# Two blocks on one core: matmuls that fill a part of the array, issued beside others on another part

## The chip, the cores and the metric

The kernel runs on one core of a Trainium2 chip. The metric is device time in microseconds (us), the median of several executions. The profile is one further execution, recorded instruction by instruction. PE is the matmul engine, PEld its weight loads, DVE, ACT and POOL the three other compute engines, SP the queue that issues the DMAs.

## The reference

Two network blocks follow each other on 256 tokens of width 1024, in float32. What the change touches, cut from the reference:

```python
m_l = silu(c) @ w_ada + b_ada                 # modulation of x, 1024 -> 6144
m_c = silu(c_ctx) @ w_ada + b_ada             # modulation of the context
u_l = modulate(x, sh1_l, sc1_l) @ w_in        # LN, scale, shift, projection; u_c likewise
...
la = log_sigmoid(r @ w_gk2 + b_gk) / 16       # decays of 4 GLA heads, r has rank 16, two directions
...
s_new = exp(b_end) * s + einsum('bhsk,bhsv->bhkv', k * exp(b_end - b), v)
o = einsum('bhts,bhsv->bhtv', scores, v) + einsum('bhtk,bhkv->bhtv', q * exp(b), s)
...
# second block, per layer l of 2, 272 rows (16 meta rows ahead of x):
y_diag = einsum('bhcls,bcshp->bclhp', cb * seg, x * dt)     # SSD mixer, 8 heads of 64
att = einsum('bhqk,bkhd->bqhd', softmax(s), v)              # FoX and MLA mixers, 4 heads of 64 each
kv = rms_norm(ckv) @ w_ukv                                  # MLA: 4 heads, 64 of k and 64 of v
```

## The kernel before

The first block reads `w_ada`, `w_in`, `w_out` and the expert tables, the second the weights of two layers (feed-forward, mixers, feed-forward). All large weights come through one stream (`class Stream`, L221): a tile of 128x1024 float32 is loaded by the SP queue into one of four `raw` buffers, and `split_to` turns it into a high part `wh` (ACT, L290) and a low part `wl` (DVE or, in mode "p", POOL, L291). A product is then three single-pass matmuls in fp32r, `mm3` at L324 to L326 (hi·hi, hi·lo, lo·hi), into PSUM banks named `main`. Mode "r" keeps the tile as it is: `ada2_step` (L598) consumes it on DVE. Smaller products are plain float32 matmuls, into four banks named `aux` (`PS()`). A float32 matmul is two instructions in the trace, one pass each.

A scheduler orders the instructions of each engine when the kernel is built; each engine then runs its list strictly in that order. Generators (`ada1_gen`, `fm_gen`, `mixer`, `ssd`, `mla`, `attention`) say which pieces may be interleaved, by the tables `FILL` and `MIX_ORDER`.

The places the change touches:

- **Modulation**, `ada1_gen` (L490). The first 2048 columns of `w_ada` are computed in four blocks n = 0..3 of 512 columns, from eight 1 MB tiles `wa`. `cs` is silu of the two condition vectors, so the stationary operand has two columns, for x and for the context. Blocks 0 and 1 are 8 float32 matmuls each (L501). Blocks 2 and 3 split six of their eight weight slices (`split`, L329 on ACT and L330 on DVE, three of 1024 columns each) and take them as fp32r pairs (L508, L509), and two as float32. ACT copies the rows out (`row`, L514), four tiny matmuls turn them to columns (L517), and DVE adds the bias into `mada` and `mctx` (L521). `modulate(1)` (L547) needs blocks 0 and 1 and makes half of the input, `xh` (ACT, L552) and `xl` (DVE, L553, L554); `modulate(3)` needs blocks 2 and 3.
- **Rank-16 gates**: `gl_gen` (L882) projects the 2x16 gate channels to `rg`, 32 partitions; `decays_g` (L896) multiplies them by `w_gk2`, four float32 matmuls (L903) with 32 rows and 512 columns, each into a bank of its own. ACT and DVE make the log-sigmoid of each (L907 to L912).
- **GLA states** in `mixer_states` (L720; L748, `nq` = 2: two heads share the partitions of a bank) and **GLA outputs** in `mixer` (L841 to L865): for each of two banks `po` (index `hp`) two heads' outputs, from the scores (`SB`, L847) and from the states (L850, 64 rows each), then square, mean, ln, exp, multiply.
- **Second block**, per layer: `ssd` output `py` (L1430), `attention` output `po` (L1518, for `mla` and for `fox`), and `mla`'s key projection (L1557). Each has heads of 64 channels: the head with odd number lies on partitions 64 to 127 of the same bank. Moving widths are 272, 144 and 16 columns (the causal blocks of 272 rows, `TT`).

Of the kernel before, what the change touches and what calls it, by code (L numbers as in the profile page):

```python
# [60 lines left out]
def layout(I):  # L61
    L = {}
# [16 lines left out]
    L["wgl"] = w[:, 4096:4128].reshape(8, 128, 32).transpose(1, 0, 2)  # L79
    wg = I["w_gk2"][0]  # L80
    z = np.zeros_like(wg[0])
    L["wgk"] = np.stack([np.concatenate([wg[0], z], 0), np.concatenate([z, wg[1]], 0)], 1)
# [87 lines left out]
def build(tc, A, out):  # L170
# [3 lines left out]
    with ExitStack() as ctx:  # L174
# [262 lines left out]
        with ExitStack() as fctx:  # L437
# [8 lines left out]
            rg = fp.tile([32, 512], F32, name="rg")  # L446
            wgk = fp.tile([32, 2, 256], F32, name="wgk")
# [31 lines left out]
            cs = const.tile([128, 2, 8], F32, name="cs")  # L479
            S.activation(out=cs, in_=vc("c2").rearrange("p (a k) -> p a k", a=2), func=AF.Silu)  # L480

            ln_exp_table()
            cp = const.tile([128, 8, 4], F32R, name="cp")
            cv_ = cp.rearrange("p k a -> p a k")
            S.activation(out=cv_[:, 0:2], in_=cs, func=AF.Copy)
            V.tensor_tensor(cv_[:, 2:4], cs, cv_[:, 0:2].bitcast(F32), OP.subtract)
            sum4 = const.tile([4, 2], F32, name="sum4")
            V.tensor_tensor(sum4, ident[0:4, 0:2], ident[0:4, 2:4], OP.add)
# [4 lines left out]
            def ada1_gen(n):  # L493
                pa = PS()
                for k in range(8):
                    if k == 4:
                        yield
                    w = wa[2 * n + k // 4]
                    c = slice(512 * (k % 4), 512 * (k % 4) + 512)
                    if n < 2 or k >= 6:  # L500
                        T.matmul(pa[0:2, :], cs[:, :, k], w[:, c], start=(k == 0), stop=(k == 7))  # L501
                        continue
                    if k % 2 == 0:
                        hi = whp.tile([128, 1024], F32R, tag="wh", name="wh")
# [5 lines left out]
                row = fp.tile([4, 512], F32, name="row", tag="gk")  # L510
                if n < 2:
                    yield
                r_ = 2 if n < 2 else 4
                S.activation(out=row[0:r_], in_=pa[0:r_, :], func=AF.Copy)  # L514
                pm = PS()
                for j in range(4):
                    T.matmul(pm[:, 2 * j:2 * j + 2], row[0:r_, j * 128:j * 128 + 128], sum4[0:r_], start=True, stop=True)  # L517
# [200 lines left out]
            def mixer_states(tg, nh, ks, a, v, sc, Sc):  # L718

                nq = 4 // nh  # L720
                for d in range(2):
# [19 lines left out]
                    for h in range(4):  # L741
# [5 lines left out]
                        for i in range(2):  # L747
                            T.matmul(o, kdT[:, i, lsl], v[:, 2 + i, 128 * h:128 * h + 128], start=(i == 0), stop=(i == 1))  # L748
# [4 lines left out]
            def mixer(tg, nh, q, ks, a, v, Sc, sc, m0, between={}):  # L753
# [84 lines left out]
                for d in range(2):  # L838
                    S.activation(out=b[d], in_=b[d], func=AF.Exp, scale=sc)
                    V.tensor_tensor(b[d], b[d], q, OP.mult)  # L840
                for hp in range(2):  # L841
                    po = PS()
                    for hh_ in range(2):
                        h = hp + 2 * hh_
                        o = po[:, 256 * hh_:256 * hh_ + 256]
# [806 lines left out]
```

## Time and profile before

| | |
|---|---|
| time, median of 3 runs (lowest, highest) | 2330.87 us (2330.6, 2331.7) |
| profiled execution: its time, its span | 2333.0 us, 2331.2 us |
| mean granted TensorE clock | 0.979 |
| busy share of PE, DVE, ACT, POOL | 96%, 67%, 50%, 23% |
| HBM read | 363.31 MB, 156 GB/s over the span |

The profiled execution took 2.1 us more than the median, of which its span leaves out 1.8. A matmul's start is measured and its end is modelled, so a PE that is "busy" is not one at its peak: the distance from start to start tells what a matmul cost.

### The profile page before, as it was taken

The numbers are of one execution on the slowest core, as the hardware profiler recorded it, in microseconds if no ns is written. First come the engines' busy times: TensorE is split into PE (matmuls) and PEld (weight loads), VectorE is DVE, ScalarE is ACT, GpSimd is POOL, SyncE is SP. The second block draws the span as 40 slices with busy tenths as digits, with TensorE's granted clock in tenths as the row PEclk, the third lists the DMA queues.
The fourth block names the chain that finished last, engine by engine and source line by source line (L and its number), as shares of the span: only waits on it lengthen the run. The fifth ranks groups of instructions, "written<-read, shape, count | busy, mean of one in ns | idle before, by whom it ended". The sixth has DMA issues, their size and how long they took to land.

```text
span 2331.2 us, 43031 instructions
## 1 busy us (share of the span) xinstructions
PE 2231.7 (96%) x17176; PEld 2130.0 (91%) x17176; DVE 1552.7 (67%) x2725; ACT 1154.7 (50%) x1983; POOL 536.5 (23%) x484
## 2 busy tenths in 40 slices
PE   8898889899999999999999998999999999899998
PEld 3787779899999999999989998889999999878998
DVE  7898868967777766555565556675556555866554
ACT  4454545344444454444455445565445444665443
POOL 2325334548666600000020003010001001302000
PEclk9998999999999999999999999999999999999999
DMA  6651224444444467555555563234564556333564
GB/s 268 200 173 64 64 82 156 145 157 152 154 153 150 151 193 229 196 187 182 181 196 172 172 180 128 91 127 145 174 182 151 172 169 193 100 98 118 183 184 125
DMA packets 101913, 367.15 MB, mean 157 GB/s; under 512 B 11440, under 2 KB 13360, under 8 KB 100432
## 3 DMA queue, kind: packets, MB, share of 16 engines
q1 hardware_dynamic: 101712, 364.41, 48.2%
q8 instruction: 134, 2.20, 0.4%
q14 instruction: 67, 0.55, 0.1%
HBM read 363.31 MB, written 1.05 MB: 156 GB/s over the span
## 4 chain that ended last, share of the span: by engine, by line
PE 81%; DVE 9%; issue 2%; ACT 2%; POOL 1%; DMA 1%; DVEq 0%; POOLq 0%; ACTq 0%
PE main L326 19%; PE main L325 19%; PE main L324 19%; PE aux L1206 5%; PE aux L1207 5%; PE aux L1208 5%; PE aux L1098 2%; DVE wl L291 1%; PE aux L818 1%; PE aux L1430 1%; PE aux L1518 1%; DVE Kt L789 1%; ACT wh L290 0%; DVE acc L384 0%; DVE cv L1339 0%
## 5 line engine op out<-in xcount | busy, mean ns | idle before, releaser
L290 ACT ACTIVATE wh<-raw 128x1024 fp32r<-128x1024 f32 (+1 forms) x630 | 659.3, 1047 | 909.7 <-PE main L325 351.1
L291 DVE TENSOR_TENSOR wl<-raw,wh 128x1024 fp32r<-128x1024 f32 (+1 forms) x573 | 705.8, 1232 | 462.7 <-ACT wh L290 461.3
L324 PE MATMUL main<-hh,wh 128*128 128x256 f32 (+1 forms) x2856 | 826.8, 291 | 20.2 <-DVE hh L421 14.4
L326 PE MATMUL main<-hh,wl 128*128 128x256 f32 (+1 forms) x2856 | 822.6, 288 | 21.1 <-DVE wl L291 17.3
L325 PE MATMUL main<-hl,wh 128*128 128x256 f32 (+1 forms) x2856 | 821.9, 288 | 1.1 <-DVE hl L425 1.0
L326 PEld LDWEIGHTS main<-hh,wl 128*128 128x128 f32 x2856 | 547.1, 192 | 25.7 <-DVE wl L291 20.0
L324 PEld LDWEIGHTS main<-hh,wh 128*128 128x128 f32 x2856 | 545.0, 191 | 25.8 <-DVE hh L421 16.5
L325 PEld LDWEIGHTS main<-hl,wh 128*128 128x128 f32 x2856 | 545.6, 191 | 3.2 <-DVE hl L425 1.8
L1207 PE MATMUL aux<-xsl,wh 128*128 128x256 f32 x1024 | 289.7, 283 | 0.0
L1208 PE MATMUL aux<-xsh,wl 128*128 128x256 f32 x1024 | 289.6, 283 | 0.0
L1206 PE MATMUL aux<-xsh,wh 128*128 128x256 f32 x1024 | 289.5, 283 | 0.0
L384 POOL TENSOR_TENSOR acc<-acc,sqk 128x272 f32<-128x272 f32 (+1 forms) x32 | 40.7, 1272 | 874.7 <-ACT sqk L379 874.4
L1092 POOL TENSOR_SCALAR oh<-cst,slotT 128x128 f32<-128x128 f32 x256 | 209.9, 835 | 91.5 <-PE aux L1098 82.9
L291 POOL TENSOR_TENSOR wl<-raw,wh 128x1024 fp32r<-128x1024 f32 (+1 forms) x57 | 150.6, 2648 | 225.1 <-ACT wh L290 221.3
L324 PE MATMUL main<-ah,wh 128*128 128x272 f32 (+1 forms) x704 | 201.7, 287 | 0.0
L325 PE MATMUL main<-al,wh 128*128 128x272 f32 (+1 forms) x704 | 201.6, 286 | 0.0
L326 PE MATMUL main<-ah,wl 128*128 128x272 f32 (+1 forms) x704 | 201.1, 286 | 0.0
L1207 PEld LDWEIGHTS aux<-xsl,wh 128*128 128x128 f32 x1024 | 196.6, 192 | 0.0
L1208 PEld LDWEIGHTS aux<-xsh,wl 128*128 128x128 f32 x1024 | 196.6, 192 | 0.0
L1206 PEld LDWEIGHTS aux<-xsh,wh 128*128 128x128 f32 x1024 | 196.4, 192 | 0.1
L326 PEld LDWEIGHTS main<-ah,wl 128*128 128x128 f32 x704 | 132.6, 188 | 0.0
L324 PEld LDWEIGHTS main<-ah,wh 128*128 128x128 f32 x704 | 132.4, 188 | 0.0
(475 smaller groups left out, 3208.4 us busy)
## 6 DMA issues: line engine op xcount, KB each, us to landing
raw<-uT SPq DMA_DIRECT2D x128, 512.0 KB, 3.3
raw<-pv SPq DMA_DIRECT2D x128, 512.0 KB, 3.5
raw<-ffn_gate SPq DMA_DIRECT2D x88, 512.0 KB, 3.4
raw<-ffn_up SPq DMA_DIRECT2D x88, 512.0 KB, 3.4
raw<-win SPq DMA_DIRECT2D x72, 512.0 KB, 3.4
raw<-ffn_down SPq DMA_DIRECT2D x64, 512.0 KB, 3.6
raw<-wa SPq DMA_DIRECT2D x32, 512.0 KB, 4.3
raw<-wout SPq DMA_DIRECT2D x24, 512.0 KB, 3.4
```

The lines of the kernel that those rows point to most:

```text
L290: S.activation(out=hi[:, :n], in_=t[:, :n], func=AF.Copy)
L291: (G if mode == "p" else V).tensor_tensor(lo[:, :n], t[:, :n], hi[:, :n].bitcast(F32), OP.subtract)
L324: T.matmul(o, lh, rh, start=start, stop=False)
L325: T.matmul(o, lh, rl, start=False, stop=False)
L326: T.matmul(o, ll, rh, start=False, stop=stop)
L384: (G if self.k < 5 else V).tensor_tensor(self.acc2, self.acc2, q, OP.add)
L789: V.tensor_tensor(K1, rb, bb1, OP.subtract)
L1092: G.tensor_scalar(oh1[:, j], iota, slotT[0][:, t0 + j:t0 + j + 1], None, op0=OP.is_equal)
L1098: T.matmul(pg[:, 128 * j:128 * j + 128], oh1[:, j], oh2[:, j], start=True, stop=True)
L1206: T.matmul(yv[d], w[0][:, c], x[0], start=st_, stop=False, skip_group_check=True)
L1207: T.matmul(yv[d], w[0][:, c], x[1], start=False, stop=False, skip_group_check=True)
L1208: T.matmul(yv[d], w[1][:, c], x[0], start=False, stop=sp_, skip_group_check=True)
```

## The change

- `ada1_gen`: all four blocks are float32 matmuls. `cs` is now 32 columns wide per k (2 used, 30 zero), and the eight products of a block go to four column groups of the array, `pa[32*(k%4) : 32*(k%4)+32]`. The splits of blocks 2 and 3 and `cp` are gone. `sum4` adds up the four groups in the small matmuls (128 rows where there were 2 or 4).
- `wgl` is stored four times side by side (128x1024 where it was 128x256; its split goes to DVE where it went to POOL), so `rg` fills 128 partitions, four copies; the four `z` matmuls read 32 rows each from a different row group, and all four banks are taken ahead of them.
- `mixer_states` and `mixer` for GLA, `ssd`, `attention`: the loop over the two heads that lie on different halves of the array becomes the innermost. The GLA outputs of both banks are made together, ahead of both epilogues.
- `mla`: two key heads in one matmul of 128 columns, evicted as two halves.

```diff
-    L["wgl"] = w[:, 4096:4128].reshape(8, 128, 32).transpose(1, 0, 2)
+    L["wgl"] = np.tile(w[:, 4096:4128].reshape(8, 128, 1, 32), (1, 1, 4, 1)).reshape(8, 128, 128).transpose(1, 0, 2)
...
-                specs.append((A["wgl"].rearrange("p k c -> p (k c)"), "p"))
+                specs.append((A["wgl"].rearrange("p k c -> p (k c)"), "s"))
...
-            cs = const.tile([128, 2, 8], F32, name="cs")
+            cs = const.tile([128, 8, 32], F32, name="cs")
+            V.memset(cs, 0.0)
...
                 for k in range(8):
                     if k == 4:
                         yield
-                    w = wa[2 * n + k // 4]
-                    c = slice(512 * (k % 4), 512 * (k % 4) + 512)
-                    if n < 2 or k >= 6:
-                        T.matmul(pa[0:2, :], cs[:, :, k], w[:, c], start=(k == 0), stop=(k == 7))
-                        continue
-                    if k % 2 == 0:
-                        hi = whp.tile([128, 1024], F32R, tag="wh", name="wh")
-                        lo = wlp.tile([128, 1024], F32R, tag="wl", name="wl")
-                        split(hi, lo, w[:, 512 * (k % 4):512 * (k % 4) + 1024])
-                    e = slice(512 * (k % 2), 512 * (k % 2) + 512)
-                    T.matmul(pa[0:4, :], cp[:, k], hi[:, e], start=(k == 0), stop=False)
-                    T.matmul(pa[0:2, :], cp[:, k, 0:2], lo[:, e], start=False, stop=False)
+                    r = slice(32 * (k % 4), 32 * (k % 4) + 32)
+                    T.matmul(pa[r], cs[:, k], wa[2 * n + k // 4][:, 512 * (k % 4):512 * (k % 4) + 512], start=(k < 4), stop=(k >= 4))
...
+                zs = [PS() for _ in range(4)]
+                for j, z in enumerate(zs):
+                    r = slice(32 * j, 32 * j + 32)
+                    T.matmul(z, wgk[r], rg[r], start=True, stop=True, tile_position=(32 * j, 0))
                 for d in range(2):
                     for f in range(2):
-                        z = PS()
-                        T.matmul(z, wgk[:, d, 128 * f:128 * f + 128], rg, start=True, stop=True)
+                        z = zs[2 * d + f]
...
+                    for hh_ in range(2):
+                        o = lambda hp: po_[hp][:, 256 * hh_:256 * hh_ + 256]
+                        for hp in hps:
+                            h = hp + 2 * hh_
+                            for i in range(2):
+                                T.matmul(o(hp), v[:, i, 128 * h:128 * h + 128], SB[:, i, h, :], start=(i == 0), stop=False)
+                        for d in range(2):
+                            for hp in hps:
+                                h = hp + 2 * hh_
+                                st = Sc[d][:, h, :] if nq == 1 else Sc[d][64 * hp:64 * hp + 64, hh_, :]
+                                T.matmul(o(hp), st, hsl(b[d], h, slice(0, 256)), start=False, stop=(d == 1))
...
-                        for hh in range(2):
-                            h = 2 * f + hh
-                            for i, (t0, n) in enumerate(TT):
+                        for i, (t0, n) in enumerate(TT):
+                            for hh in range(2):
+                                h = 2 * f + hh
                                 T.matmul(py[64 * hh:64 * hh + 64, t0:], xdt[0:n, i, 64 * h:64 * h + 64], E[i][0:n, h], start=(i == 0), stop=(i == 2))
...
-                    for h in range(4):
+                    for h in range(0, 4, 2):
                         p = PS()[:, 0:272]
-                        T.matmul(p[0:64], wukv[:, l, 64 * h:64 * h + 64], ckv, start=True, stop=True)
-                        S.activation(out=mk[0:64, h], in_=p[0:64], func=AF.Copy)
-                        yield
+                        T.matmul(p, wukv[:, l, 64 * h:64 * h + 128], ckv, start=True, stop=True)
+                        for e in range(2):
+                            S.activation(out=mk[0:64, h + e], in_=p[64 * e:64 * e + 64], func=AF.Copy)
+                            yield
```

Line numbers of the changed kernel are larger by 2 to 9 (L501 stays, L517 becomes L508, L324 becomes L326, L847 becomes L842, L850 becomes L847, L1430 becomes L1438).

**PE, end of the modulation.** `wa` is a weight tile, `cs` and `cp` the condition columns, `row` the copied rows, `main` the first projection. Before, blocks 1, 2 and the beginning of the projection:

```order
L501 MATMUL aux<-wa,cs 2x512 x2
L517 MATMUL aux<-sum_148,row 128x2 x4
L508 MATMUL aux<-wh,cp 4x512
L509 MATMUL aux<-wl,cp 2x512
L508 MATMUL aux<-wh,cp 4x512
L509 MATMUL aux<-wl,cp 2x512
L508 MATMUL aux<-wh,cp 4x512
L324 MATMUL main<-xh,wh 128x512 x2
L325 MATMUL main<-xl,wh 128x512
```

Now, from the end of the first 24 projection matmuls:

```order
L328 MATMUL main<-xh,wl 128x512
L501 MATMUL aux<-wa,cs 32x512 x7
L326 MATMUL main<-xh,wh 128x512
L327 MATMUL main<-xl,wh 128x512
L328 MATMUL main<-xh,wl 128x512
L326 MATMUL main<-xh,wh 128x512
L508 MATMUL aux<-sum_146,row 128x2 x4
L501 MATMUL aux<-wa,cs 32x512 x8
L327 MATMUL main<-xl,wh 128x512
```

One matmul of block 2 stands ahead of the projection; its other seven and all eight of block 3 stand behind 24 projection matmuls, with no split between them.

**PE, SSD outputs of a layer.** `E0` to `E2` and `xdt` are the operands of a head's three matmuls; a bank `aux` holds two heads. Before:

```order
L1430 MATMUL aux_16585<-E0_16350,xdt_16349 64x272
L1430 MATMUL aux_16585<-E1_16351,xdt_16349 64x144
L1430 MATMUL aux_16585<-E2_16352,xdt_16349 64x16
L1430 MATMUL aux_16585<-E0_16350,xdt_16349 64x272
L1430 MATMUL aux_16585<-E1_16351,xdt_16349 64x144
L1430 MATMUL aux_16585<-E2_16352,xdt_16349 64x16
```

Now a bank's six matmuls, and further down the attention outputs of FoX:

```order
L1438 MATMUL aux_16549<-E0_16314,xdt_16313 64x272 x2
L1438 MATMUL aux_16549<-E1_16315,xdt_16313 64x144 x2
L1438 MATMUL aux_16549<-E2_16316,xdt_16313 64x16 x2
...
L1526 MATMUL aux_17174<-foxT0_16874,fv_16322 64x272 x2
L1526 MATMUL aux_17182<-foxT0_16874,fv_16322 64x272
L1526 MATMUL aux_17174<-foxT1_16875,fv_16322 64x144 x2
L1526 MATMUL aux_17174<-foxT2_16876,fv_16322 64x16 x2
L1526 MATMUL aux_17182<-foxT0_16874,fv_16322 64x272
```

Equal widths of the two heads now stand side by side; of FoX's second bank the two wide ones are apart.

**PE, GLA outputs.** `stg0` and `stg1` are the states, `bl0` and `bl1` the decayed queries, the two `aux` numbers the two banks. Now:

```order
L842 MATMUL aux_2418<-SB_1941,v_gl_947 128x256
L842 MATMUL aux_2419<-SB_1941,v_gl_947 128x256
L842 MATMUL aux_2418<-SB_1941,v_gl_947 128x256
L842 MATMUL aux_2419<-SB_1941,v_gl_947 128x256
L847 MATMUL aux_2418<-bl0_1935,stg0_1906 128x256
L847 MATMUL aux_2419<-bl0_1935,stg0_1906 128x256
L847 MATMUL aux_2418<-bl1_1938,stg1_1933 128x256
L847 MATMUL aux_2419<-bl1_1938,stg1_1933 128x256
```

Before, one bank's eight came first, with projection matmuls between them, then its epilogue beside the other bank's eight; now sixteen stand in a row and both epilogues behind them.

## Rows read from the trace of the kernel before

**Rows 1.** Page, part 1: busy us (share of the span) and instructions of each engine.

```profile
PE 2231.7 (96%) x17176; PEld 2130.0 (91%) x17176; DVE 1552.7 (67%) x2725; ACT 1154.7 (50%) x1983; POOL 536.5 (23%) x484
```

**Rows 2.** Windows: stretch, length, busy PE, PEld, DVE, ACT, POOL, clock, DMA share, GB/s.

```profile
35.00:45.00 10.00, 9.07 (x30) 4.63 (x28) 10.00 (x15) 5.90 (x10) 5.99 (x7) 0.85 0.33 114
140.00:180.00 40.00, 36.98 (x245) 31.43 (x245) 39.97 (x44) 18.62 (x27) 19.36 (x9) 1.00 0.44 143
192.50:196.10 3.60, 3.60 (x4) 1.15 (x4) 2.40 (x5) 2.31 (x5) 1.67 (x1) 0.50 0.00 0
1482.00:1514.00 32.00, 31.97 (x185) 21.83 (x186) 16.85 (x38) 14.38 (x45) 0.00 (x0) 1.00 0.18 58
1514.00:1546.00 32.00, 31.05 (x228) 27.51 (x227) 21.87 (x46) 23.80 (x67) 0.00 (x0) 1.00 0.39 124
```

**Rows 3.** DMA issues of the first 40 us: KB each, median us from issue to landing.

```profile
wa<-wa SPq DMA_DIRECT2D x7, 1024.0 KB, 17.5
```

**Rows 4.** Timeline of the modulation: start us, us, engine, line, instruction [idle before].

```profile
34.84 0.41 DVE L553 TENSOR_SCALAR xm<-xn,mada 128x256 f32<-128x256 f32 x1
...
37.59 1.21 DVE L330 TENSOR_TENSOR wl<-wa,wh 128x1024 fp32r<-128x1024 f32 x1
...
42.68 1.66 DVE L330 TENSOR_TENSOR wl<-wa,wh 128x1024 fp32r<-128x1024 f32 x1
...
44.27 0.68 DVE L554 TENSOR_TENSOR xl<-xm,xh 128x512 fp32r<-128x512 f32 x1
...
46.37 1.88 PE L501 MATMUL aux<-wa,cs 128*2 128x512 f32 x4
...
55.08 0.57 ACT L514 ACTIVATE row<-aux 4x512 f32<-4x512 f32 x1
...
55.20 1.23 DVE L590 TENSOR_TENSOR crow<-crow,sg 128x1024 f32<-128x1024 f32 x1 [0.60 <-ACT sg L589]
...
56.16 1.05 PE L517 MATMUL aux<-sum,row 4*128 4x2 f32 x8
...
57.24 0.16 DVE L521 SCALAR_TENSOR_TENSOR mada<-aux,vec 128x4 f32<-128x4 f32 x1 [0.81 <-PE aux L517]
```

**Rows 5.** PE alone, two short windows of its timeline: part-array matmuls already side by side.

```profile
247.62 1.09 PE L748 MATMUL aux<-v_gl,kdT 128*64 128x128 f32 x14
...
262.77 1.16 PE L818 MATMUL aux<-Qt,Kt 64*128 64x128 f32 x16 [0.98 <-POOL Qt L806]
```

**Rows 6.** Window of L1567 alone (32 columns, 272 moving): length, busy PE, PEld, clock, DMA.

```profile
1501.97:1502.66 0.69, 0.67 (x9) 0.16 (x8) 1.00 0.00 0
```

**Rows 7.** Chain of waits in layer 0's mixers: start us, us, what.

```profile
1493.34 1.98 PE aux L1557 x8
...
1509.30 4.31 PE aux L1518 x24
...
1538.87 4.31 PE aux L1518 x24
```

**Rows 8.** Groups of PE by line: busy us, mean ns of one.

```profile
L1430 PE MATMUL aux<-E,xdt 128*64 128x272 f32 (+2 forms) x96 | 18.1, 308 | 0.0
```

**Rows 9.** Timeline of the gate rank: projection's split, then two of the z matmuls.

```profile
140.81 1.00 POOL L291 TENSOR_TENSOR wl<-raw,wh 128x256 fp32r<-128x256 f32 x1 [23.54 <-ACT wh L290]
...
191.71 1.33 DVE L826 COPY_PREDICATED SB<-msk,aux 128x512 f32<-128x512 uint8 x2
192.49 3.78 PE L903 MATMUL aux<-rg,wgk 32*128 32x512 f32 x4 [1.81 <-DVE SB L826]
```

**Rows 10.** Timeline of the GLA outputs, bank 0, and its epilogue on ACT.

```profile
294.46 1.13 PE L850 MATMUL aux<-bl,stg 64*128 64x256 f32 x4
295.63 0.60 ACT L852 ACTIVATE o<-aux 128x512 f32<-128x512 f32 x1 [8.24 <-PE aux L850]
```

**Rows 11.** Chain of waits, end of the GLA outputs: start us, us, what.

```profile
300.39 1.06 PE aux L850 x4
...
306.71 0.62 PE main L324 x3
```

More of the change, by code (lines that the diff above doesn't have):

```diff
@@ L78, in layout @@
     L["win"] = np.concatenate(gs, 0)
-    L["wgl"] = w[:, 4096:4128].reshape(8, 128, 32).transpose(1, 0, 2)
+    L["wgl"] = np.tile(w[:, 4096:4128].reshape(8, 128, 1, 32), (1, 1, 4, 1)).reshape(8, 128, 128).transpose(1, 0, 2)
     wg = I["w_gk2"][0]
     z = np.zeros_like(wg[0])
-    L["wgk"] = np.stack([np.concatenate([wg[0], z], 0), np.concatenate([z, wg[1]], 0)], 1)
+    wg = (np.concatenate([wg[0], z], 0), np.concatenate([z, wg[1]], 0))
+    L["wgk"] = np.concatenate([wg[d][:, 128 * f:128 * f + 128] for d in range(2) for f in range(2)], 0)
     L["wout"] = I["w_out"][0].reshape(8, 128, 8, 128).transpose(2, 1, 0, 3).reshape(8, 128, 1024)
@@ L445, in build @@
             xctx = tl("xctx", [8, 256], "v_gl")
-            rg = fp.tile([32, 512], F32, name="rg")
-            wgk = fp.tile([32, 2, 256], F32, name="wgk")
+            rg = fp.tile([128, 512], F32, name="rg")
+            wgk = fp.tile([128, 128], F32, name="wgk")
             gat = [tl(f"gat{d}", [2, 4, 256]) for d in range(2)]
@@ L476, in build @@
             W.dma_to(3)
-            cs = const.tile([128, 2, 8], F32, name="cs")
-            S.activation(out=cs, in_=vc("c2").rearrange("p (a k) -> p a k", a=2), func=AF.Silu)
+            cs = const.tile([128, 8, 32], F32, name="cs")
+            V.memset(cs, 0.0)
+            S.activation(out=cs[:, :, 0:2].rearrange("p k a -> p a k"), in_=vc("c2").rearrange("p (a k) -> p a k", a=2), func=AF.Silu)
             ln_exp_table()
[L483 to L488, printed above, removed]
+            sum4 = const.tile([128, 2], F32, name="sum4")
+            V.tensor_tensor(sum4, ident[:, 0:2], ident[:, 32:34], OP.add)
+            V.tensor_tensor(sum4, sum4, ident[:, 64:66], OP.add)
+            V.tensor_tensor(sum4, sum4, ident[:, 96:98], OP.add)
             mada = const.tile([128, 48], F32, name="mada")
@@ L740, in mixer_states @@
                     pst = PS()
-                    for h in range(4):
+                    for h, i in [(h0 + e, i) for h0 in range(0, 4, nq) for i in range(2) for e in range(nq)]:
                         if nq == 1:
@@ L746, in mixer_states @@
                             lsl = slice(64 * h, 64 * h + 64)
-                        for i in range(2):
-                            T.matmul(o, kdT[:, i, lsl], v[:, 2 + i, 128 * h:128 * h + 128], start=(i == 0), stop=(i == 1))
+                        T.matmul(o, kdT[:, i, lsl], v[:, 2 + i, 128 * h:128 * h + 128], start=(i == 0), stop=(i == 1))
                     st = tl(f"st{tg}{d}", [nh, 128], f"st{d}")
@@ L1514, in attention @@
                         po = PS()[:, 0:272]
-                        for hh in range(2):
-                            h = 2 * f + hh
-                            for j, (s0, m) in enumerate(TT):
+                        for j, (s0, m) in enumerate(TT):
+                            for hh in range(2):
+                                h = 2 * f + hh
                                 T.matmul(po[64 * hh:64 * hh + 64, s0:], v[0:m, j, 64 * h:64 * h + 64], PT[j][0:m, h], start=(j == 0), stop=(j == 2))
```

31 lines of the change are left out of this document (15 added, 16 removed).

## The prediction

> **What bounds the kernel now.** I read the engine totals first [rows 1]: PE is busy for 2231.7 of 2331.2 us, so most of what PE no longer has to do comes off the end. That is an average, so I then read windows of the stages that the change touches [rows 2]. From 35 to 45 us DVE is busy for 10.00 of 10.00 us and PE has holes; from 140 to 180 us DVE has 39.97 of 40.00 and PE 36.98; in the mixers of the second block PE has 31.97 of 32 and then 31.05 of 32, with DVE at 16.85 and 21.87 and ACT at 14.38 and 23.80. So a shorter PE list pays one for one in the second block, by DVE's list only at the end of the modulation, and hardly at all in the stretch of the gate rank.
>
> The second question is whether two matmuls on different parts of the array do run together. The kernel before already has such neighbours [rows 5]: in L748 two heads share a bank by columns (64 of 128), and 14 instructions take 1.09 us; in L818 heads lie on 64 rows each, and 16 take 1.16 us. L1567 has four heads of 32 columns with 272 moving: its eight instructions, two for each of four matmuls, fill 0.67 us of one window [rows 6]. Against that, L1557 with the same width, 64 columns and no neighbour on the other half, takes 1.98 us for eight [rows 7], 0.25 each. One after another L1567 would have needed 1.98 too, so four column groups ran at a third of the serial time, and the two passes of 0.25 that are left, with a first one a little longer, make up the 0.67. I take half the serial time for pairs, and about 0.05 us extra where the shape changes.
>
> **The sum, part by part**, against the profiled execution (2333.0 us; the median lies 2.1 lower).
>
> *Front, −5.3.* The eight `wa` tiles are 17.5 us from issue to landing [rows 3], issued one behind the other, so the early blocks wait for them, and faster matmuls there gain nothing. `modulate(1)` starts on DVE at 34.84 [rows 4], behind other DVE work; I leave it there. Behind it two splits on DVE go away, 1.21 + 1.66 = 2.87 us [rows 4], so the last `xl`, done at 44.27 + 0.68 = 44.95, is done at about 42.1. Now PE: five projection matmuls (1.1, at the 0.62 for three of [rows 11]) and the seven of block 2. In [rows 4] two matmuls of L501, four instructions, took 1.88 us, 0.94 each. A quad side by side costs one of those, so the seven cost 1.88: 45.1. Four projection matmuls cover the copy of the row (0.9 and 0.57); then the small ones of L517, 1.05: 47.0. Block 3 the same again: 1.88, the row 0.57 and a hand-over, L517 1.05: 50.6 for the last `mada`, 57.24 before [rows 4]. That is 6.6 earlier. But `crow` (DVE, 1.23) was done beside block 3 and now falls behind `modulate(3)`: 5.3 is left. For the bounds: if block 3 waits for something of DVE all the same, 2; if also `modulate(1)` comes forward, because DVE has fewer small operations ahead, 11. `cs` gets 32 columns and a memset, ahead of the first weights: hidden by their 17.5 us.
>
> *Gate-rank weights, +1.2.* The split of `wgl` is 1024 wide where it was 256 and goes to DVE, where POOL took 1.00 [rows 9]. A DVE operation of that width takes 1.21 [rows 4]. DVE is full here [rows 2], so I count all of it; 0 if a hole takes it, +2 if it collides with POOL like the 1.66. The projection's 24 matmuls fill 128 columns where they filled 32, with the same moving width: 0. Another 384 KB come through the stream, 0.1% of the 363 MB: 0.
>
> *Decays, −1.4.* Two of the four `z` wait for banks that L826 on DVE holds until 191.71 + 1.33 = 193.0, and then two matmuls take 3.78 us [rows 9], at a granted clock of 0.50, that is 1.2 GHz [rows 2]. Side by side they take half of that, 1.9, to which I add 0.5 for the first: from 3.78 to 2.4. At the higher clock it would be 2.6 less. ACT and DVE take the four `z` in turn, so it may also hide: 0.
>
> The Trainium skill ("TensorE: Matmul & The Clock Gate", Part 3, the measured speedups) has four matmuls on four row groups at 3.07 times the speed of one after another, not four times. By that, two `z` would fall by less than half, and an estimate for the four is 7.56 / 3.07 = 2.5 us.
>
> *GLA states, 0.* The heads of L748 already overlap [rows 5]; the new nesting changes their order alone.
>
> *GLA outputs, −3.0.* Now bank 0 ends at 294.46 + 1.13 = 295.6, its epilogue starts on ACT at 295.63 [rows 10], bank 1's last products end at 300.39 + 1.06 = 301.5, and the projection returns at 306.71 [rows 11]: PE waits 5.2 us for the epilogue of bank 1. In the changed order all sixteen products stand in a row, and the projection matmuls that stood between them move into that wait. The eight state products in pairs cost half: four groups of two, 1.1 each [rows 10, 11] fall by 2.2, and some ten changes of shape give 0.5 back. Both banks should be done at about 295.7. But both epilogues stand behind them now, 5.2 for the second and some 2.6 more for the first on the same engines: the projection returns at about 303.5, 3.2 earlier, of which I keep 3.0. Bounds: +1.5, if the epilogues follow each other in full; −4.6, if the first one costs nothing more.
>
> *Second block, −18.2 for both layers.* SSD's outputs L1430 take 18.1 us in 96 instructions, eight banks of 2.26 [rows 8]; in pairs 9.05 less. MLA's twelve matmuls of L1518 take 4.31, in pairs −2.15 [rows 7]. FoX's take 4.31 too [rows 7], but in its second bank one wide pair is split up in the order: −1.65. The four key projections, 1.98 [rows 7], become two: −0.99. Per layer 4.52 + 2.15 + 1.65 + 0.99 = 9.3; both 18.6, less 0.4 for changes of shape. PE is the limit here [rows 2], so all of it counts. Bounds: −19.5, if a shape costs nothing; −14.5, if ACT holds some back (below).
>
> For this term too there is a rule: the same page and section of the Trainium skill gives 2.38 times for three matmuls on three column groups. An estimate by that, some 1.6 times for two, would make this term about −15; the 0.67 of [rows 6] speaks for less loss, three times for four.
>
> Sum: −5.3 + 1.2 − 1.4 − 3.0 − 18.2 = −26.7, so 2306.3 in the profiled execution's terms and 2304 for the median.
>
> **The rivals.** *ACT takes over in the second mixers* (B). In the second half of a layer's mixers ACT is busy for 23.80 of 32 us [rows 2], with softmax and the copies of the keys, which stay eight. PE's list there gets 3.7 us shorter per layer (attention and keys), and where ACT's chain is full, half of that is lost: −26.7 + 3.7 gives 2308, and with the front at its small bound of −2, 2311.5. Against it: 23.80 of 32 leaves a quarter free.
>
> *The front gives more* (C). The full DVE stretch [rows 2] is fed by PE's blocks 0 and 1. If `modulate(1)` starts some 3.4 us earlier, as blocks 0 and 1 now cost a quarter, the front gives −9: 2300. Against it: the 17.5 us of [rows 3], and POOL and DVE are both busy from 35 to 45 us.
>
> *Column neighbours run one after another* (D, the other side). Then the fp32 matmuls of the modulation, which replace cheaper split ones, would cost 15 × 0.94 = 14.1 us where I count 3.8: the front gives +5 for −5.3. `wgl` still costs 1.2, the outputs lose the epilogue that lay beside bank 1, +1.5, `z` gives 0, and the second block keeps only the keys, −2.0: 2333.0 + 5.7 − 2.1 = 2336.6. It decides from the point where a quad takes more than about 2.3 us, since then block 2 and block 3 eat the 5.3. For it speaks only the page named above, in the part on the mechanism: a weight load overlaps running matmuls only where the row group is another, and two column neighbours have the same rows. By that rule the time is the 2336.6 of this rival. [Rows 5, 6] show column neighbours together, so the trace disagrees with so strict a reading.
>
> **How the numbers follow.** The forecast with its terms within their bounds 0.66, B 0.17, C 0.14, D 0.03. The range runs from the ends of the terms that are most open: 2293 is the front at −11, the decays at −2.6, outputs at −4.6 and the second block at −19.5, with 0 for `wgl`; 2317 is the front at −2, the outputs at +1.5, `wgl` at +2 and the second block at −14.5, some 13 less than before. Both hold A, B and C but for their tails, together about 0.15, and D. A measurement here can tell about 0.2%, 4.7 us, from no change. A, B and C lie 19 us or more below 2330.87; only tails of B with outputs and front both lost come within 4.7, 0.02; D gives slower, 0.03; faster 0.95.
>
> **What would show it.** In the changed profile the last `mada` should stand at about 50.6, with L501 in steps of 0.9 for four; if it stands at 55 or later, look for what DVE or a weight tile holds. The group of SSD outputs should fall from 18.1 to about 9, the attention outputs from 4.31 to about 2.2 (FoX 2.7), the keys from 1.98 to 1.0. The `z` should take about 2 us for the last two, GLA's last output should end at about 295.7, and the projection return at about 303.5. ACT as the one that ends PE's waits in the mixers would speak for B, a `modulate(1)` near 31.4 for C, and SSD outputs still at 18 for D. The prediction is wrong if a pair costs more than some 0.7 of its serial time, or if the time saved on PE turns into waits for DVE or ACT behind it.

## The result, and the profile after

| | before | after |
|---|---|---|
| time, median (lowest, highest) | 2331.28 us (2330.6, 2333.78) | 2304.69 us (2302.7, 2307.95) |
| profiled execution: span | 2331.2 us | 2300.9 us |
| mean granted TensorE clock | 0.979 | 0.978 |

The ratio is 0.9885, with a 95% interval of 0.9868 to 0.9903: 26.6 us less, where 26.7 were worked out. The two profiled executions lie further apart than the medians, 30.3 us, because that of before was 1.7 above its median and that of after 2.0 below; the last section says where such differences arise.

Part 1 of the page of after answers to [rows 1]: PE lost 42.3 us of busy time, which is more than the kernel lost. Most of the rest lies in the first blocks of the modulation: in the first 35 us PE was busy for 24.97 us before and for 16.92 after, and DVE's part of the first modulation starts at the same time, since it waits for DVE in both.

```profile
PE 2189.4 (95%) x17168; PEld 2116.5 (92%) x17168; DVE 1547.5 (67%) x2722; ACT 1148.5 (50%) x1976; POOL 534.2 (23%) x483
```

The timeline of after at the modulation, and at the gate rank's products, answers to [rows 4, 9] (start us, us, engine, line, operation; L562 scales the normalised input):

```profile
27.41 6.15 POOL L562 TENSOR_TENSOR xctx<-xctx,rstd 128x1024 f32<-128x1024 f32 x2 [26.97 <-ACT rstd L336]
...
27.98 6.66 DVE L562 TENSOR_TENSOR xn<-xn,rstd 128x1024 f32<-128x1024 f32 x2
...
30.30 1.09 ACT L543 ACTIVATE xh<-xctx,mctx 128x256 fp32r<-128x256 f32 x2 [2.97 <-POOL xctx L562]
...
34.57 0.70 DVE L544 TENSOR_SCALAR xm<-xn,mada 128x256 f32<-128x256 f32 x1
...
41.12 0.94 DVE L545 TENSOR_TENSOR xl<-xm,xh 128x512 fp32r<-128x512 f32 x1
...
44.25 1.92 PE L501 MATMUL aux<-wa,cs 128*32 128x512 f32 x14
...
47.99 1.92 PE L501 MATMUL aux<-wa,cs 128*32 128x512 f32 x16
...
51.88 0.16 DVE L512 SCALAR_TENSOR_TENSOR mada<-aux,vec 128x4 f32<-128x4 f32 x1 [2.42 <-PE aux L508]
...
60.99 1.21 DVE L581 TENSOR_TENSOR crow<-crow,sg 128x1024 f32<-128x1024 f32 x1
...
181.62 1.13 PE L908 MATMUL aux<-rg,wgk 32*128 32x512 f32 x4
188.15 2.68 PE L908 MATMUL aux<-rg,wgk 32*128 32x512 f32 x4 [5.39 <-DVE SB L816]
```

The first modulation starts on DVE at 34.57 and its last `xl` is done at 42.06, as forecast. (On ACT it starts at 30.30, where the trace of before has 34.84; what PE then waits for is `xl`.) Eight products of a block take 1.92 us. The last `mada` lands at 51.88 for 57.24, and `crow` now stands behind the second modulation.

The windows of after for these stretches (columns as in [rows 2]):

```profile
32.00:41.00 9.00, 5.05 (x11) 3.52 (x12) 9.00 (x12) 2.44 (x5) 6.70 (x8) 0.50 0.58 237
41.00:44.00 3.00, 3.00 (x14) 2.36 (x13) 0.96 (x2) 0.00 (x0) 1.16 (x2) 0.96 0.02 5
...
188.10:190.80 2.70, 2.65 (x5) 1.04 (x5) 2.25 (x4) 1.49 (x3) 1.72 (x1) 0.50 0.00 0
...
322.40:329.30 6.90, 6.89 (x32) 5.92 (x32) 3.42 (x10) 4.74 (x12) 2.30 (x4) 1.00 0.04 17
...
1499.60:1523.20 23.60, 23.55 (x187) 21.71 (x183) 19.02 (x39) 21.16 (x59) 0.00 (x0) 1.00 0.49 157
```

From 32 to 41 us the granted clock is 0.50, 1.2 GHz; PE had waited 5.64 us for ACT just before, and waits another 3.92 for DVE inside. In the last window, the second half of layer 0's mixers, ACT is busy for 21.16 of 23.60 us, and PE still for 23.55: ACT is close, but holds nothing.

The chain of waits of after, at two loads, at the GLA outputs and in layer 0's mixers, answers to [rows 7, 11]:

```profile
95.14 5.75 DMA raw<-wa
...
130.68 4.17 DMA raw<-wa
...
289.20 1.11 PE aux L847 x8
290.31 0.59 ACT o L855
...
296.78 0.39 PE main L327
...
1473.38 2.30 PE aux L1438 x24
...
1480.36 0.92 PE aux L1565 x4
...
1494.01 2.22 PE aux L1526 x24
...
1520.58 2.66 PE aux L1526 x22
```

Eight of the GLA's state products, on two halves of the rows, take 1.11 us, where four took 1.06 in [rows 11]. The keys take 0.92 for 1.98, MLA's outputs 2.22 for 4.31, FoX's 2.66 for 4.31 (the view merges all but two of its 24 instructions). The group of SSD outputs stands at 9.8 us for the 18.1 of [rows 8]:

```profile
L1438 PE MATMUL aux<-E,xdt 128*64 128x272 f32 (+2 forms) x96 | 9.8, 310 | 0.0
```

Between the two profiles I followed the same projection matmul from stage to stage. After is earlier by 6.0 us behind the products of block 3 (57.71 against 51.70), by 6.2 behind the gate rank (201.91 against 195.74), by 8.0 behind the GLA outputs (306.71 against 298.68), by 9.4 at the start of the second block (1229.49 against 1220.13), by 20.6 behind layer 0's mixers (1577.43 against 1556.85) and by 29.9 behind layer 1's (2100.88 against 2071.02). So two thirds come from the second block. Its two ends, before:

```profile
1229.49 0.39 PE L326 MATMUL main<-hh,wl 128*128 128x272 f32 x1 [0.53 <-DVE wl L291]
...
2100.88 0.39 PE L326 MATMUL main<-mh,wl 128*128 128x272 f32 x1
```

And after:

```profile
1220.13 0.40 PE L328 MATMUL main<-hh,wl 128*128 128x272 f32 x1 [0.23 <-DVE wl L293]
...
2071.02 0.39 PE L328 MATMUL main<-mh,wl 128*128 128x272 f32 x1
```

### The profile page after: what moved, and what is told of

Same layout as the page of the kernel before. It is cut to its first block, busy times and chain, and to the rows that moved or that the text cites. A ratio compares the mean times of both kernels' runs of the same rounds, so it can differ in the third digit from the quotient of the medians.

```text
span 2300.9 us, 42996 instructions
## 1 busy us (share of the span) xinstructions
PE 2189.4 (95%) x17168; PEld 2116.5 (92%) x17168; DVE 1547.5 (67%) x2722; ACT 1148.5 (50%) x1976; POOL 534.2 (23%) x483
## 4 chain that ended last, share of the span: by engine, by line
PE 83%; DVE 9%; issue 3%; POOL 2%; DMA 1%; ACT 1%; SPq 0%; DVEq 0%; POOLq 0%; ACTq 0%
PE main L328 20%; PE main L327 20%; PE main L326 20%; PE aux L1214 5%; PE aux L1215 5%; PE aux L1216 5%; PE aux L1106 2%; DVE wl L293 1%; DMA raw<-wa 1%; POOL wl L293 1%; DVE raw L589 1%; PE aux L808 1%; DVE acc L386 0%; PE aux L1526 0%; PE aux L1438 0%
## 5 line engine op out<-in xcount | busy, mean ns | idle before, releaser
L326 PE MATMUL main<-hh,wh 128*128 128x256 f32 (+1 forms) x2856 | 826.7, 290 | 20.2 <-DVE hh L423 14.4
L326 PEld LDWEIGHTS main<-hh,wh 128*128 128x128 f32 x2856 | 545.6, 191 | 25.3 <-DVE hh L423 16.5
L326 PE MATMUL main<-ah,wh 128*128 128x272 f32 (+1 forms) x704 | 201.9, 287 | 0.0
L293 POOL TENSOR_TENSOR wl<-raw,wh 128x1024 fp32r<-128x1024 f32 x56 | 151.2, 2704 | 214.5 <-ACT wh L292 203.5
L326 PEld LDWEIGHTS main<-ah,wh 128*128 128x128 f32 x704 | 132.6, 188 | 0.0
```

What stands on the lines that cost most here:

```text
L293: (G if mode == "p" else V).tensor_tensor(lo[:, :n], t[:, :n], hi[:, :n].bitcast(F32), OP.subtract)
L326: T.matmul(o, lh, rh, start=start, stop=False)
```

## The experiments

Each kernel ran beside the kernel before on the same chip, in three groups. There the kernel before took 2332.08 us (the second block undone, the modulation undone, and the two with one group of columns), 2335.03 (same half, gate rank, GLA outputs, half scaled first) and 2333.47 (the rest). So differences within a group count, and terms of one or two us are read from the traces. Of these groups only the third holds the changed kernel itself; in the first, a kernel's distance to the kernel before is set against the 26.6 us of the result, and in the second, where the kernel before was slowest, the gate rank undone serves as the neighbour.

**The second block's part undone** (and everything else kept):

```diff
-                        for i, (t0, n) in enumerate(TT):
-                            for hh in range(2):
-                                h = 2 * f + hh
+                        for hh in range(2):
+                            h = 2 * f + hh
+                            for i, (t0, n) in enumerate(TT):
                                 T.matmul(py[64 * hh:64 * hh + 64, t0:], ...
...
-                    for h in range(0, 4, 2):
+                    for h in range(4):
```

> The second block's part alone is undone (SSD and attention outputs head after head, four key matmuls of 64 columns). Theory (neighbours on different halves run together and PE is the limit there): the whole part comes back, 18 to 21 us, so 2323 to 2326; 24 instructions of SSD outputs take 4.3 to 4.4 us for 2.30, MLA's 24 take 4.3 for 2.22, the keys 1.98 for 0.92. Rival (ACT holds part of the mixers): less than half to two thirds comes back, 2314 to 2318, and ACT ends PE's waits in the changed kernel. Rival (the sum was right by luck, and the first block gave most): under 12 us, below 2317.

2325.66 us (2323.72 to 2326.9), ratio 0.997 (0.9958 to 0.9982): 6.4 below the kernel before, where the changed kernel is 26.6 below: about 20 came back. Its chain has the old durations in the same places:

```profile
1478.78 4.39 PE aux L1438 x24
...
1488.89 1.98 PE aux L1565 x8
...
1504.85 4.31 PE aux L1526 x24
```

The theory stands; the two rivals, two thirds or less, fall.

**The same part alone**, on top of the kernel before:

```diff
-                        for hh in range(2):
-                            h = 2 * f + hh
-                            for j, (s0, m) in enumerate(TT):
+                        for j, (s0, m) in enumerate(TT):
+                            for hh in range(2):
+                                h = 2 * f + hh
                                 T.matmul(po[64 * hh:64 * hh + 64, s0:], ...
...
-                    for h in range(4):
+                    for h in range(0, 4, 2):
```

> The kernel before with the second block's part of the change alone (SSD, attention, keys). Theory: 18 to 21 us under the kernel before. Together with the modulation alone this leaves 0 to 4 of the whole for the GLA outputs and the gate rank. Rival (parts interact): the two sums miss the whole by more than 5.

2314.97 us, ratio 0.9921 (0.9907 to 0.9934): 18.5 below the kernel before, as expected.

**The modulation alone**, on top of the kernel before:

```diff
-                    T.matmul(pa[0:4, :], cp[:, k], hi[:, e], start=(k == 0), stop=False)
-                    T.matmul(pa[0:2, :], cp[:, k, 0:2], lo[:, e], start=False, stop=False)
+                    r = slice(32 * (k % 4), 32 * (k % 4) + 32)
+                    T.matmul(pa[r], cs[:, k], ...
```

> The kernel before with the modulation's part of the change alone. Theory: the part is worth the same alone as together with the others, 4 to 6 us under the kernel before. Rival (it only pays together with the others): under 2.

2326.65 us, ratio 0.9972 (0.9963 to 0.9982): 6.8 below, a little more than the 4 to 6 expected. The last `mada` stands at 51.19. And **the changed kernel again**, without an edit, in the same group:

> The changed kernel once more, beside the next three on the same chip, since the kernel before differs by up to 4 us from one chip to the next. Theory: 26 to 27 us under the kernel before of this call, within 2. Its profile also tells which of two things recur: the state additions of the first layer normalisation's sums (32 matmuls) take 6.81 us in some profiles and 8.5 in others; if that is chance it may fall either way, and the first block differs by up to 3 us between profiles of the same program.

2305.59 us, ratio 0.988 (0.9864 to 0.9895): 27.9 below. The two parts alone make 25.3, so 2.6 are left for the outputs and the gate rank: the parts add up.

**The modulation undone**:

```diff
-                    r = slice(32 * (k % 4), 32 * (k % 4) + 32)
-                    T.matmul(pa[r], cs[:, k], ...
+                    if n < 2 or k >= 6:
+                        T.matmul(pa[0:2, :], cs[:, :, k], w[:, c], start=(k == 0), stop=(k == 7))
+                        continue
+                    if k % 2 == 0:
+                        split(hi, lo, ...
```

> The modulation alone is undone (two-column operand, splits of blocks 2 and 3). Theory: the last column of block 3 lands at about 57 us for 51.9, and the time rises by 4.5 to 6, so 2309 to 2311. Rival (the loads of the modulation's later columns, which the changed kernel waits for between 80 and 105 us, took back part of the gain): 2 to 3.5 us, so 2307 to 2308.

2309.37 us, ratio 0.9905 (0.989 to 0.992): 22.7 below the kernel before, where the changed kernel is 26.6 below, so 3.9 came back. The last `mada` stands at 58.44, 6.6 later than in the changed kernel. The 3.9 lie between what the theory and the rival expected, and this measurement can't part them.

**One group of columns for all products**:

```diff
-                    r = slice(32 * (k % 4), 32 * (k % 4) + 32)
+                    r = slice(0, 32)
```

> The modulation stays without splits, but all eight products of a block go to one group of 32 columns, one after another. Theory (side by side is what pays): a block takes about 6.9 us for 1.85; blocks 2 and 3 together add some 10 us ahead of the last column, which lands at 61 to 63; the time rises by 9 to 11, so 2314 to 2316, worse than the undone modulation. Rival (the gain comes from the splits that DVE no longer does, and PE has room): 0 to 3 us, so 2305 to 2308. Rival (blocks 0 and 1 also bind): more than 12 us, above 2317.

2310.3 us, ratio 0.9908 (0.9893 to 0.9923). The price of a block is as expected, what comes of it is not. Its timeline:

```profile
50.50 7.05 PE L502 MATMUL aux<-wa,cs 128*32 128x512 f32 x16
...
51.09 1.23 DVE L583 TENSOR_TENSOR crow<-crow,sg 128x1024 f32<-128x1024 f32 x1 [0.25 <-ACT sg L582]
52.34 1.22 DVE L591 SCALAR_TENSOR_TENSOR raw<-raw,crow 128x1024 f32<-128x1024 f32 x1
...
54.64 1.22 DVE L591 SCALAR_TENSOR_TENSOR raw<-raw,crow 128x1024 f32<-128x1024 f32 x1
...
59.71 0.16 DVE L514 SCALAR_TENSOR_TENSOR mada<-aux,vec 128x4 f32<-128x4 f32 x1 [3.84 <-PE aux L510]
```

One after another the sixteen instructions of a block take 7.05 us for 1.92, 3.7 times as long, and the last `mada` comes 7.8 us later. The kernel is 21.8 below the kernel before, so 4.8 of the 7.8 reach the end, and it is no faster than the modulation undone beside it (0.9 slower): without neighbours side by side the new modulation gains nothing. The expected 9 to 11 had not counted what DVE does meanwhile: it uses the wait for `crow` and three consuming steps, 4.9 us, which in the changed kernel stand behind the modulation. That this is what took the rest back is likely, but no run removes it.

**Blocks 0 and 1 alone in one group**:

```diff
-                    r = slice(32 * (k % 4), 32 * (k % 4) + 32)
+                    one = n < 2
+                    r = slice(0, 32) if one else slice(32 * (k % 4), 32 * (k % 4) + 32)
```

> Blocks 0 and 1 go to one group of 32 columns, blocks 2 and 3 stay side by side. In the changed kernel PE idles 5.6 us ahead of the projection and runs its first ten matmuls at half clock (0.43 us each, granted 0.50). Theory (the idle time costs clock, and nothing else hangs on blocks 0 and 1): the granted clock from 32 to 41 us stays near 1.0, the 24 first projection matmuls end 0.5 to 1.2 us earlier, and so does the last column: 2303.5 to 2304.5. Rival (blocks 0 and 1 release the first modulated tiles): these start later than 34.6, and the time rises by 1 to 4, 2306 to 2309. Rival (nothing hangs on either): the same within 0.5.

2306.26 us, ratio 0.9891 (0.9876 to 0.9906). The first theory falls: PE still waits ahead of the projection, and its clock from 36 to 41 us is 0.56.

```profile
32.59 3.37 DVE L293 TENSOR_TENSOR wl<-raw,wh 128x1024 fp32r<-128x1024 f32 x1
...
37.21 1.22 PE L326 MATMUL main<-xh,wh 128*128 128x512 f32 x2 [2.92 <-ACT xh L545]
```

Block 1's `mada` starts at 35.89, the first modulation 1.5 us later than in the changed kernel, at 36.07, and the last `mada` stands at 53.68. That is what the first rival expected, but not for its reason alone: block 1's small products end at 33.30, and DVE is then in a split of 3.37 us. The kernel is 25.8 below the kernel before for 26.6, which this measurement can't tell from no difference. What the half clock costs stays open, since this kernel didn't remove it.

**SSD neighbours on the same half**:

```diff
-                            for hh in range(2):
-                                h = 2 * f + hh
+                                for e_ in range(2):
+                                    h = 2 * (f0 + e_) + hh
```

> SSD outputs alone: equal widths still stand side by side, but the two neighbours are heads of two banks that lie on the same half of the array. Theory (different halves are what pays): neighbours start 0.23 us apart, as in the kernel before, not 7 ns; the first 24 instructions take 4.2 to 4.4 us for 2.30; the time rises by 6 to 9, so 2311 to 2314. Rival (what pays is that equal widths follow each other, or that two banks are open): starts a few ns apart and 2.3 us, the same time as the changed kernel, 2304 to 2306.

2309.61 us, ratio 0.9893 (0.9876 to 0.9909). The first 24 instructions are the clean case, as in the further ones the scheduler put some different halves side by side:

```profile
1476.90 3.83 PE L1439 MATMUL aux<-E,xdt 128*64 128x272 f32 x24
```

They take 3.83 us, where the changed kernel has 2.37 in the same view. Neighbours of 272 columns start 0.229 us apart here; in the second part, where different halves met, 0.013. The time is 4.8 above the gate rank undone beside it, less than the 6 to 9 expected, and the 3.83 us lie below the expected 4.2 to 4.4. So the half is what pays, with one correction: the first 24 took 4.39 in head order, in the chain of the first experiment, and take 3.83 here, because equal widths follow each other. In head order a step from 144 to 16 columns takes 0.216 us and one between two of 16 takes 0.079, in the trace of the first experiment; here there are half as many steps between widths. That is 0.28 us a bank, an eighth, which needs no second half.

**The gate rank undone**:

```diff
-                zs = [PS() for _ in range(4)]
-                for j, z in enumerate(zs):
-                    T.matmul(z, wgk[r], rg[r], start=True, stop=True, tile_position=(32 * j, 0))
...
+                        z = PS()
+                        T.matmul(z, wgk[:, d, 128 * f:128 * f + 128], rg, start=True, stop=True)
```

> The gate rank alone is undone (weights once, their split on POOL, four products of 32 rows one after another). Theory (two small terms of opposite sign, 1.2 on DVE and 1.4 on PE): within 1.5 of the changed kernel, 2303.5 to 2306.5; the last two products take 3.7 us again for 2.7. Rival (the wider split on DVE costs more than the products give): 1 to 3 us faster, 2302 to 2304. Rival (the products were on the path): 2 to 4 us slower, 2307 to 2309.

2304.85 us, ratio 0.9875 (0.9858 to 0.9891), where the theory expected it: nothing is lost, and a small gain can't be excluded, since the changed kernel did not run in this group. Its timeline has the old price:

```profile
187.54 3.78 PE L905 MATMUL aux<-rg,wgk 32*128 32x512 f32 x4 [1.03 <-DVE SB L815]
```

The changed kernel saves 1.1 of this 3.78, and its wider split goes to DVE; that the two cancel is not shown one by one.

**The GLA outputs undone**:

```diff
-                if nq == 2:
-                    outputs((0, 1))
                 for hp in range(2):
-                    if nq == 1:
-                        outputs((hp,))
-                    po = po_[hp]
+                    po = PS()
+                    for hh_ in range(2):
+                        h = hp + 2 * hh_
+                        ...
```

> The GLA outputs alone are undone (bank by bank, each ahead of its epilogue). Theory: from the first output of bank 0 to the projection's return at layer normalisation some 1.5 to 3 us more, time 2306 to 2308. Rival (the epilogue that lay beside bank 1 was worth as much as the pairs): within 0.5, 2304.5 to 2305.5.

2307.2 us, ratio 0.9886 (0.987 to 0.9903), 2.4 above the gate rank undone beside it. The chain:

```profile
287.29 1.06 PE aux L840 x4
...
295.26 1.06 PE aux L840 x4
...
301.60 0.62 PE main L326 x3
```

Against the changed kernel's profile it is about 1 us behind ahead of the outputs (278.58 against 279.51), and 2.9 behind after them (298.68 against 301.60). So the outputs cost about 2 more here; counted from the score products ahead of them (L808, 279.64 against 281.18) it is 1.4. Of the 2.4 in the time, 1.7 can be the clock at the sums that follow (last section). The rival falls by the trace, and the term is 1.4 to 2.

**Half of the input scaled first, all of it on DVE**, on top of the changed kernel:

```diff
-                        (G if e and st is rstd else V).tensor_tensor(xn[e][:, a:a + 4], ...
+                        if a == 0 or st is mean:
+                            V.tensor_tensor(xn[e][:, a:a + 4], ...
...
             modulate(1)
+            for e in range(2):
+                V.tensor_tensor(xn[e][:, 4:8], xn[e][:, 4:8], ..., OP.mult)
```

> On top of the changed kernel: of the normalised input only the half that the first modulation needs is scaled ahead of it, both for x and the context on DVE; the other half is scaled behind it, and POOL does none. In the changed kernel two such operations take 6.66 us on DVE beside 6.15 on POOL, where one alone took 1.22. Theory (DVE is held by POOL's work beside it, and the first modulation hangs on it): the first modulation starts at 30 to 31 us for 34.57, the last column lands at 48 to 49 for 51.88, and the time falls by 2.5 to 4, so 2300.5 to 2302. Rival (the loads of the later modulation columns pace the stretch from 78 to 106 us anyhow): the columns come earlier, but the time falls by less than 1, 2304 to 2305. Rival (PE's half clock grows): the first projection matmuls run longer at 0.43 us each and give back 1 to 2.

2303.39 us, ratio 0.9867 (0.985 to 0.9883): 1.5 below the gate rank undone beside it, and between what the theory and the first rival expected. The timeline shows what held DVE:

```profile
28.14 1.22 DVE L563 TENSOR_TENSOR xn<-xn,rstd 128x1024 f32<-128x1024 f32 x1
29.28 1.22 DVE L563 TENSOR_TENSOR xctx<-xctx,rstd 128x1024 f32<-128x1024 f32 x1
30.41 0.72 DVE L544 TENSOR_SCALAR xm<-xn,mada 128x256 f32<-128x256 f32 x1
...
49.55 0.16 DVE L512 SCALAR_TENSOR_TENSOR mada<-aux,vec 128x4 f32<-128x4 f32 x1 [2.40 <-PE aux L508]
```

The same operation takes 1.22 us where POOL scales nothing, and 3.33 on average beside POOL's scaling in the changed kernel. The first modulation starts at 30.41, 4.2 us earlier, and the last `mada` at 49.55, 2.3 earlier. To see whether the time follows, it was run **together with the undone gate rank**, beside the changed kernel:

> The changed kernel with half of the input scaled ahead of the first modulation (as in the run before) and the gate rank undone. Theory (both remove DVE work ahead of a stretch where DVE is full, or stand on no path): 2 to 4 us under the changed kernel of the same call. Rival (the later columns' loads and DVE's list take the early start back): within 1.

2305.8 us (2300.94 to 2307.05) against 2305.59 for the changed kernel: no difference, as the rival said. The traces show where the 2.3 us are lost: the same projection matmul stands at 49.37 for 51.70 behind block 3 in the run with half scaled first, at 195.18 for 195.74 behind the gate rank, and at 298.81 for 298.68 behind the GLA outputs. No kernel here is shown to beat the changed one.

## Why the prediction was right, point by point

The forecast was 2304 and the result 2304.69. The likeliest case came true, and mostly by its own terms. That the sum, 26.7 us, meets the measured 26.6 within 0.1 is luck: the changed kernel again was 27.9 below the kernel before, and single terms were off by one or two us in both directions.

- **Do neighbours run together?** Yes. Of the rivals, "one after another" (D) would have left the SSD outputs at 18.1; they stand at 9.8, and only neighbours on different halves do it. MLA's twelve products went from 4.31 to 2.22, 1.94 times, where the estimate from the Trainium skill ("TensorE: Matmul & The Clock Gate", Part 3, the measured speedups), which has 2.38 times for three column groups, was 1.6; the rows were the better guide. The sentence of the Trainium skill (same page, Part 3, the mechanism) that a load overlaps only with other row groups, read strictly, is contradicted by these column neighbours: in layer 0 two of MLA's products on the same rows start 7 ns apart, and the second one's load lies beside the first one's matmul. D also had its price too high: it counted 10.3 us for a modulation one after another, and the run with one group of columns lost 4.8.
- **Second block, −18.2:** measured −18.5 alone, about −20 when undone. The terms per layer are 4.2 for SSD by halves of 9.8 and 18.1 (4.5 forecast), 2.1 for MLA, 1.65 for FoX, 1.06 for the keys, 9.0 together; by the projection matmuls around them (1480.04 to 1560.01 before, 1470.20 to 1540.07 after) layer 0 gained 10.1. Most of the rest are shorter waits of PE: 31.05 of 32.00 us busy in [rows 2], 23.55 of 23.60 now. ACT as the new limit (B) didn't come: ACT has 21.16 of those 23.60 us. B's own sum was a little low: attention and keys are 4.8 us per layer by the prediction's terms, not 3.7, so B stood for some 2309.
- **Front, −5.3:** 3.9 when undone and 6.8 when added alone, with the last `mada` 5.4 earlier between the two profiles and 6.6 against the modulation undone, whose scaling starts at 27.89, as in the changed kernel (27.98); that of before started at 26.93. It should have stood at 50.6. The step that failed is the five projection matmuls behind the last `xl` at 0.21 each: PE was at 1.2 GHz until 41 us and had more of them left, so block 2 began at 44.25 where 43.2 was reckoned, and the copy and hand-over of block 3 cost the rest.
- **The first modulation "behind other DVE work":** the time was right and the reason incomplete. In the timeline of before, a third split stands ahead of it, 3.37 us from 31.36 (the rows below the list), which the text didn't count; now the scaling of the input, held by POOL, ends at the same time. That is also why C, the earlier start, didn't come; when it was brought about, the time didn't follow.
- **Gate rank, +1.2 and −1.4:** together nothing can be measured. The first two of the four products do run side by side (1.13 us, at a granted clock of 1.00), but the last two stand at 2.68 instead of the 2.4 forecast, since they start 0.6 us apart as their banks come free, at 1.2 GHz. That the 384 KB more are always hidden, as the 0 for them says, is not shown (last section).
- **GLA outputs, −3.0:** −1.4 to −2. The last output was forecast at 295.7 in the frame of before; less the 6 us gained ahead of it that is 289.7, and it ended at 290.31. The epilogues of both banks then took 6.5 us until the projection went on at 296.78, 1.3 less than the 7.8 reckoned. But the matmul that goes on there is not the one at 306.71 of before: 15 projection matmuls, which had stood between the outputs, come first, at 0.12 each, and the same matmul stands at 298.68. The forecast had let them all go into the wait.

The rows of before at the scaling of the input and the third split:

```profile
26.93 1.22 DVE L571 TENSOR_TENSOR xn<-xn,rstd 128x1024 f32<-128x1024 f32 x1 [0.28 <-ACT rstd L334]
...
26.98 6.67 POOL L571 TENSOR_TENSOR xctx<-xctx,rstd 128x1024 f32<-128x1024 f32 x2 [26.54 <-ACT rstd L334]
...
28.64 2.80 DVE L571 TENSOR_TENSOR xn<-xn,rstd 128x1024 f32<-128x1024 f32 x1
...
31.36 3.37 DVE L330 TENSOR_TENSOR wl<-wa,wh 128x1024 fp32r<-128x1024 f32 x1
```

## What to carry to other kernels

Where PE is the limit, let matmuls that use half the rows or half the columns alternate between the halves, with equal widths next to each other: 64-column pairs gained 1.94 times here for a change of loop order alone, and four groups of 32 columns 3.7 times. Where another engine is the limit, price the change by what that engine can do meanwhile: of 7.8 us by which the modulation came later, 4.8 reached the end, while DVE did work that it had to do anyway, and 2.3 us by which it came earlier were not seen in the time. Measure one part alone and the same part undone, and let both agree before a term is believed.

## What the runs showed that was not expected

**The same program takes 5 us more or less in its first 250 us.** The same projection matmul stands at 151.44 in the first profile of the changed kernel and at 155.11 in the second, a later one at 250.87 and 256.14, and from there on they stay 3.8 to 5.5 us apart. The first one's chain waits for a tile `wa` 5.75 us from 95.14 and 4.17 us from 130.68 (the first lines of the chain above). The second one's chain:

```profile
95.48 7.05 DMA raw<-wa
...
133.44 6.88 DMA raw<-wgl
```

So the waits for these two are 4.0 us longer, and 3.7 of the difference stand there by 151 us. Weight tiles of 512 KB are on the two chains with 3.2 to 7.1 us, but for one piece of 1.1. The tile `wgl`, which the change made four times as large, is on the chain in the second profile with 6.88 us. The forecast had its transfer at 0. It lands 3.3 to 3.8 us after its issue in the five profiles where it has 128 KB, and 4.3 to 6.9 in the nine where it has 512, but it is on the chain in this one of the nine alone; in the modulation alone, with 128 KB, the chain waits 6.07 us for a `win` tile at 132.35. So whether the larger tile costs time is open.

**The clock after an idle stretch differs from run to run.** The 32 sum matmuls at the first layer normalisation, behind 3.1 us without work for PE in every profile, took 6.81 us in eight of the fourteen profiles of this study, about 8.5 in three, that of before among them, and about 9.7 in three. The windows of the changed kernel above have them at 322.40 with a clock of 1.00. The window of the GLA outputs undone:

```profile
325.50:334.10 8.60, 8.57 (x32) 7.09 (x32) 3.43 (x11) 4.85 (x12) 2.32 (x4) 0.80 0.04 17
```

That is 1.7 of the 30.3 us between the profiles shown. The second block undone, whose first block is that of the changed kernel, took 8.5, so the order of instructions does not decide it. But all eight profiles with 6.81 are of kernels with the new order of the GLA outputs, and none of the four with the old order is among them. Whether the change has a part in it stays open.

**DVE stands still beside POOL.** The 1024-wide scaling took 1.22 us alone and 3.33 beside a POOL operation of 3.08. The Trainium skill ("SBUF — State Buffer", Terms, shared port pair) says that the two engines hold a pair of ports in turn, for a whole instruction; these numbers agree with it, though no run here took the ports themselves apart. Which one starts first matters: in the rows of before above, DVE's operation that started 0.05 us ahead of POOL's took 1.22, and the next, started while POOL's ran, 2.80.
